# Every fourth weight chunk gets its lower part from an accumulating transfer instead of a VectorE subtraction

## The chip, the cores and the metric

The kernel runs on one core of one Trainium2 chip. The metric is the device time of one execution in microseconds (us). The core has a matrix engine (TensorE; PE for its matmuls and PEld for its weight loads in the profile), a vector engine (VectorE, DVE), a scalar engine (ScalarE, ACT), GpSimd (POOL) and SyncE (SP). SP, ACT and POOL can issue transfers (DMAs); these are carried by sixteen DMA engines between the chip's main memory and the on-chip buffers.

## The reference

The reference computes two layers of a decoder trunk on 256 rows of 2048 channels. Each layer normalizes `x`, multiplies it with one wide input matrix, feeds the pieces to four token mixers (causal pooling, latent attention with a rotary key, a gated short convolution, cross-attention to 256 memory rows), projects each mixer's output, merges the four with sigmoid gates, and adds an output projection to `x`. Cut to the parts that hold nearly all the arithmetic:

```python
for l in range(DEPTH):                       # DEPTH = 2
    h = rms_norm(x, norm_g[l])               # (256, 2048)
    proj = h @ w_in[l]                       # (2048, 18496)
    ...                                      # four mixers, with their own smaller products
    mem_kv = rms_norm(mem, mem_norm_g[l]) @ w_mem_kv[l]
    merged = gates[:, :, 0] * (y_pool @ w_branch[l, 0])
    merged = merged + gates[:, :, 1] * (y_mla @ w_branch[l, 1])
    merged = merged + gates[:, :, 2] * (y_conv @ w_branch[l, 2])
    merged = merged + gates[:, :, 3] * (y_mem @ w_branch[l, 3])
    x = x + merged @ w_out[l]
```

All inputs and outputs are 32-bit floats.

## The kernel before

Every large product is done with operands split in two. A number is written as an upper part, rounded to the type `float32r` in which TensorE takes it, and a lower part, the difference between the number and its upper part. A product of two such numbers is then formed from three matmuls (upper by upper, upper by lower, lower by upper).

The weights lie in main memory in chunks, in the order in which they are used. `wchunks` (lines 293 to 306) is a generator that brings one chunk at a time: SP loads it as 128 partitions of up to 1024 numbers into a buffer `raw` (line 303), ACT rounds it into `hi` (line 304, `A.copy`), and DVE subtracts, `lo = raw - hi` (line 305). There are four buffers for `raw`, three for `hi` and three for `lo`. The load, the rounding and the subtraction stand in a block of higher priority (`AHEAD`, 100 places in the program's order), so that they are put ahead of other work in the queues of their engines; they then wait for their buffers.

Two helpers use the chunks. `tm_block` (lines 308 to 320) has the activations as the stationary operand and the weights as the moving one; a chunk of 2 by 512 columns costs twelve matmuls, four times the lines 317, 318 and 319, and line 318 is the one that reads `lo`. `fm_block` with `fm_tile` (lines 322 to 333) has the weights stationary; a chunk of 4 by 256 columns costs eight pairs of the lines 323 and 324, and line 324 loads `lo`. A whole block is 16 k-tiles deep for most products: eight chunks in `tm_block`, four in `fm_block`. Both accumulate in `acc`, of which there are three buffers.

A run goes through 884 chunks, 442 in each layer: the key and value projection of the memory rows, the latents, the cross-attention queries, an order of attention stages written out by hand (`SEQUENCE`, line 22), then for each branch in turn the gate and branch projections (`gates`), with the pooling branch and the convolution branch between them, and the output projection. Of the 884, 836 hold 128 by 1024 numbers; 32 (the compressed keys and values) hold 128 by 576 and 16 (`uq`) hold 128 by 768.

Intermediate results of up to 128 by 1152 numbers live in buffers of the tag `t4` (lines 132 and 133), of which the pool `tp` (line 121) has seven. POOL does no arithmetic; it clears the first columns of one tile per pooling group (line 738) and per convolution half (line 783).

Of the kernel before, what the change touches and what calls it, by code (L numbers as in the profile page):

```python
# [10 lines left out]
F32 = mybir.dt.float32  # L11
F32R = mybir.dt.float32r
I32 = mybir.dt.int32
AF = mybir.ActivationFunctionType
ALU = mybir.AluOpType
AX = mybir.AxisListType

P = 128
# [92 lines left out]
def tile_hybrid_trunk(  # L111
    ctx: ExitStack, tc: tile.TileContext, x, xT, mem, memT, positions, vectors, mla_g, gate_b, weights, consts, out,
):
    nc = tc.nc
    V, A, T = nc.vector, nc.scalar, nc.tensor
# [2 lines left out]
    big = ctx.enter_context(tc.tile_pool(name="big", bufs=2))  # L118
    wp = ctx.enter_context(tc.tile_pool(name="wp", bufs=1))
    op = ctx.enter_context(tc.tile_pool(name="op", bufs=16))  # L120
    tp = ctx.enter_context(tc.tile_pool(name="tp", bufs=7))
    sp = ctx.enter_context(tc.tile_pool(name="sp", bufs=4))
    accp = ctx.enter_context(tc.tile_pool(name="accp", bufs=3, space=bass.MemoryType.PSUM))
    msp = ctx.enter_context(tc.tile_pool(name="msp", bufs=2, space=bass.MemoryType.PSUM))
# [3 lines left out]
    def nm(s):  # L128
        uid[0] += 1
        return f"{s}{uid[0]}"  # L130
# [147 lines left out]
    def step():  # L278
        if background:
            run = background.pop(0)  # L280
            if run is not None:
                run()
# [5 lines left out]
    def defer(runs, delay):  # L288
        if len(background) < delay:
            background.extend([None] * (delay - len(background)))  # L290
        background.extend(runs)

    def wchunks(l, name, c0):
        off, n, nk, kt = plan[name, c0]
        m = nk * n
        for k0 in range(0, kt, nk):
            raw = wp.tile([P, 1024], F32, tag="raw", name=nm("raw"), bufs=4)
            hi = wp.tile([P, 1024], F32R, tag="hi", name=nm("hi"), bufs=3)
            lo = wp.tile([P, 1024], F32R, tag="lo", name=nm("lo"), bufs=3)
            o = off + P * n * k0  # L300
            step()
            with tc.high_priority(AHEAD):
                nc.sync.dma_start(raw[:, :m], weights[l, o : o + P * m].rearrange("(p m) -> p m", p=P))
                A.copy(hi[:, :m], raw[:, :m])  # L304
                V.tensor_tensor(lo[:, :m], raw[:, :m], hi[:, :m].bitcast(F32), ALU.subtract)  # L305
            yield k0, nk, kt, n, *(w[:, :m].rearrange("p (k n) -> p k n", n=n) for w in (hi, lo))

    def tm_block(lhs, l, name, c0):
        ps = acc()
        for k0, nk, kt, n, hi, lo in wchunks(l, name, c0):  # L310
            for k in range(nk):
                kk = k0 + k
                o = lhs(kk // 2) if callable(lhs) else lhs[kk // 2]
                for t in range(2):
                    hh = o[:, kk % 2, 0, t * P : (t + 1) * P]
                    hl = o[:, kk % 2, 1, t * P : (t + 1) * P]
                    T.matmul(ps[:, t, :n], hh, hi[:, k, :], start=kk == 0, stop=False)  # L317
                    T.matmul(ps[:, t, :n], hh, lo[:, k, :], start=False, stop=False)  # L318
                    T.matmul(ps[:, t, :n], hl, hi[:, k, :], start=False, stop=kk == kt - 1)  # L319
        return ps  # L320
# [5 lines left out]
    def fm_block(rhs, l, name, c0):  # L326
        ps = acc()
        for k0, nk, kt, n, hi, lo in wchunks(l, name, c0):
            for j in range(2):
                for k in range(nk):  # L330
                    kk = k0 + k
                    fm_tile(ps, j, hi, lo, rhs[kk // 2], kk % 2, k, j * P, kk == 0, kk == kt - 1)
        return ps
# [396 lines left out]
    def pool_branch(l, vec, h):  # L730
# [24 lines left out]
        for b in range(2):  # L755
            sz = silu_block(h, l, OFF["pz"] + 512 * b)
            (_, _, _, _, hi, lo), = wchunks(l, "pool", 512 * b)
            for i in range(2):
                g = 2 * b + i
                ps = acc()  # L760
                for j in range(2):
                    for k in range(2):
                        fm_tile(ps, j, hi, lo, mixed[g], k, 2 * i + k, j * P, k == 0, k == 1)
                y = t2("yp").rearrange("p (n s) -> p n s", n=2)
                fm_sum(y, ps)
                for j in range(2):
                    V.scalar_tensor_tensor(
                        y[:, j, :], y[:, j, :], gcol(vec, "pool_scale", 2 * g + j), sz[:, 2 * i + j, :], ALU.mult, ALU.mult
                    )
                o = opnd()  # L770
                split(o, y)
                ys.append(o)
# [89 lines left out]
    for l in range(DEPTH):  # L862
# [45 lines left out]
        o, sz = xq, sxz  # L908
# [75 lines left out]
```

## Time and profile before

| | |
|---|---|
| Median of two runs | 2519.72 us |
| Lowest and highest | 2518.49 and 2520.94 us |
| Span of the profiled execution | 2517.2 us |
| The profiled execution's own time | the page gives only its span, so the 2.5 us to the median of the runs are counted as what lies around it |
| PE busy | 2503.9 us, 12402 matmuls |
| DVE busy, ACT busy | 1539.0 us and 1248.4 us |
| POOL busy | 1.6 us, 16 instructions |
| Transfers | 484.22 MB, 192 GB/s on average |
| Granted TensorE clock | full speed |

The page of a profile gives, for each engine, the time in which it worked and its share of the span; then groups of instructions by line of the source, with the mean duration of one instruction in ns and the idle time that the engine had just before them, with what ended that wait. `A <- B` behind a group means that A's instruction could start when B was done. In a timeline, each row has the start in us, the duration in us, the engine, the line, the operation with its output and inputs, and in square brackets the idle time before it. A matmul's row is longer than the distance to the next one, because matmuls overlap in the array. The rows themselves are shown where the prediction uses them.

### The profile page before, as it was taken

The page shows a single profiled execution, that of the slowest core. Times are in us where ns is not written, and L with a number is a line of the kernel's source. Part 1 is how long each engine was busy: PE and PEld are TensorE (multiplying, and loading weights), DVE is VectorE, ACT ScalarE, POOL GpSimd, SP SyncE. Part 2 cuts the span into 40 slices and gives each one's busy share as a digit, 9 for nine tenths or more (in the row PEclk, how much of TensorE's full clock was granted, in tenths as well). Part 3 has the DMA queues.
Part 4 walks back from the last instruction along what each step waited for, and adds up shares of the span by engine and source line. Part 5 has one row for each costly group of instructions (what it writes and reads, how often), then busy time and mean ns, then how long its engine had stood idle before and what let it go on. Part 6 is the DMA issues. An engine that isn't in the chain of part 4 may idle for free.

```text
span 2517.2 us, 32451 instructions
## 1 busy us (share of the span) xinstructions
PE 2503.9 (99%) x12402; PEld 2108.3 (84%) x12402; DVE 1539.0 (61%) x2132; ACT 1248.4 (50%) x1707; POOL 1.6 (0%) x16
## 2 busy tenths in 40 slices
PE   8999999999999999999999999999999999999999
PEld 7888888888888888888888888888888888888887
DVE  6767775566556655556474577755765565555554
ACT  7556674445444444445454566744444444444443
POOL 0000000000000000000000000000000000000000
PEclk9999999999999999999999999999999999999999
DMA  8665436655655566667655654366556655566565
GB/s 314 207 198 162 145 128 197 202 188 192 201 196 186 188 221 203 201 195 231 220 187 167 202 166 136 128 202 204 186 191 202 194 187 188 193 202 203 189 229 164
DMA packets 143676, 484.22 MB, mean 192 GB/s; under 512 B 16160, under 2 KB 17184, under 8 KB 143520
## 3 DMA queue, kind: packets, MB, share of 16 engines
q1 hardware_dynamic: 142800, 481.06, 58.5%
q8 instruction: 97, 1.59, 0.3%
q10 hardware_dynamic: 720, 1.09, 0.1%
q14 instruction: 59, 0.48, 0.1%
HBM read 477.89 MB, written 4.19 MB: 192 GB/s over the span
## 4 chain that ended last, share of the span: by engine, by line
PE 97%; DVE 1%; ACT 1%; DMA 0%; issue 0%; DVEq 0%; SPq 0%; ACTq 0%
PE acc L319 22%; PE acc L318 22%; PE acc L317 22%; PE acc L323 19%; PE acc L324 10%; PE ms L703 1%; PE ms L702 1%; PE ms L350 1%; DVE lo L305 0%; ACT junk L197 0%; PE ms L551 0%; PE ms L552 0%; PE ms L553 0%; DMA row<-in_x_dram 0%; ACT hi L304 0%; PE ms L722 0%
## 5 line engine op out<-in xcount | busy, mean ns | idle before, releaser
L305 DVE TENSOR_TENSOR lo<-raw,hi 128x1024 fp32r<-128x1024 f32 (+2 forms) x884 | 1062.4, 1202 | 869.8 <-ACT hi L304 867.0
L304 ACT CAST hi<-raw 128x1024 fp32r<-128x1024 f32 (+2 forms) x884 | 914.7, 1035 | 1179.1 <-PE acc L319 791.2
L317 PE MATMUL acc<-hi,op 128*128 128x512 f32 (+2 forms) x2496 | 962.5, 386 | 5.8 <-ACT op L392 5.7
L318 PE MATMUL acc<-lo,op 128*128 128x512 f32 (+2 forms) x2496 | 957.9, 384 | 1.7 <-DVE lo L305 1.7
L319 PE MATMUL acc<-hi,op 128*128 128x512 f32 (+2 forms) x2496 | 958.1, 384 | 0.0
L323 PE MATMUL acc<-op,hi 128*128 128x512 f32 x2080 | 736.9, 398 | 0.1
L324 PE MATMUL acc<-op,lo 128*128 128x256 f32 x2080 | 585.7, 282 | 0.0
L317 PEld LDWEIGHTS acc<-hi,op 128*128 128x128 f32 x2496 | 469.2, 188 | 95.2 <-ACT op L392 6.2
L319 PEld LDWEIGHTS acc<-hi,op 128*128 128x128 f32 x2496 | 469.0, 188 | 92.0 <-issue 1.3
L318 PEld LDWEIGHTS acc<-lo,op 128*128 128x128 f32 x2496 | 469.4, 188 | 91.1 <-DVE lo L305 2.9
L323 PEld LDWEIGHTS acc<-op,hi 128*128 128x128 f32 x2080 | 390.8, 188 | 94.3 <-DVE z L338 0.8
L324 PEld LDWEIGHTS acc<-op,lo 128*128 128x128 f32 x2080 | 392.9, 189 | 1.9 <-issue 1.3
L814 DVE TENSOR_TENSOR g<-acc,gb 128x1024 f32<-128x1024 f32 x32 | 39.2, 1224 | 12.7 <-PE acc L319 12.7
L337 ACT COPY fmt<-acc 128x512 f32<-128x512 f32 x72 | 41.4, 581 | 0.0
L815 ACT ACTIVATE g<-g 128x1024 f32<-128x1024 f32 x32 | 34.0, 1062 | 6.7 <-DVE g L814 6.7
L821 DVE TENSOR_TENSOR g<-g,acc 128x1024 f32<-128x1024 f32 x24 | 29.3, 1221 | 9.8 <-PE acc L319 9.8
L822 DVE TENSOR_TENSOR merged<-merged,g 128x1024 f32<-128x1024 f32 x24 | 29.2, 1219 | 0.0
L513 ACT ACTIVATE sm<-sm,smx,rqs 128x128 f32<-128x128 f32 (+1 forms) x32 | 17.3, 540 | 22.3 <-DVE smx L511 22.3
L494 DVE TENSOR_TENSOR z<-z,sg 128x512 f32<-128x512 f32 x32 | 22.0, 688 | 7.8 <-ACT sg L493 7.7
L197 ACT ACTIVATE junk<-acc 128x256 f32<-128x256 f32 (+2 forms) x68 | 25.2, 371 | 2.1 <-PE acc L319 1.2
L392 ACT ACTIVATE op<-ms,gt 128x256 fp32r<-128x256 f32 x32 | 15.1, 471 | 14.0 <-DVE op L393 14.0
L338 DVE TENSOR_TENSOR z<-acc,fmt 128x512 f32<-128x512 f32 x32 | 21.9, 684 | 0.0
(193 smaller groups left out, 949.1 us busy)
## 6 DMA issues: line engine op xcount, KB each, us to landing
raw<-in_weights_dram SPq DMA_DIRECT2D x836, 512.0 KB, 3.5
raw<-in_weights_dram SPq DMA_DIRECT2D x32, 288.0 KB, 2.8
gb<-in_gate_b_dram SPq DMA_DIRECT2D x32, 256.0 KB, 4.4
raw<-in_weights_dram SPq DMA_DIRECT2D x16, 384.0 KB, 3.1
mt<-in_memT_dram SPq DMA_DIRECT2D x14, 256.0 KB, 5.7
row<-in_mem_dram SPq DMA_DIRECT2D x4, 512.0 KB, 8.4
row<-in_x_dram SPq DMA_DIRECT2D x4, 512.0 KB, 8.2
xt<-in_xT_dram SPq DMA_DIRECT2D x8, 256.0 KB, 5.5
```

The source lines that it names most:

```text
L304: A.copy(hi[:, :m], raw[:, :m])
L305: V.tensor_tensor(lo[:, :m], raw[:, :m], hi[:, :m].bitcast(F32), ALU.subtract)
L317: T.matmul(ps[:, t, :n], hh, hi[:, k, :], start=kk == 0, stop=False)
L318: T.matmul(ps[:, t, :n], hh, lo[:, k, :], start=False, stop=False)
L319: T.matmul(ps[:, t, :n], hl, hi[:, k, :], start=False, stop=kk == kt - 1)
L323: T.matmul(ps[:, j, :], hi[:, k, n0 : n0 + P], o[:, half].rearrange("p a s -> p (a s)"), start=first, stop=False)
L324: T.matmul(ps[:, j, :S], lo[:, k, n0 : n0 + P], o[:, half, 0, :], start=False, stop=last)
L337: A.copy(tmp, ps[:, :, S:])
L814: V.tensor_tensor(g, pg, gb.unsqueeze(1).broadcast_to([P, 2, 512]), ALU.add)
L815: A.activation(g, g, AF.Sigmoid)
L821: V.tensor_tensor(g, g, pb, ALU.mult)
L822: V.tensor_tensor(mg, mg, g, ALU.add)
```

## The change

The chunks are counted. Where the count is a multiple of four and the chunk has the full 1024 columns, `lo` is made in another way: ACT writes the negated chunk into `lo`, which rounds it, so that it holds the negated upper part; then POOL issues a transfer that reads the same chunk from main memory a second time and adds it to what stands in `lo`. The result is again the chunk less its upper part. All other chunks keep the subtraction on DVE. The buffers are dealt out anew: three for `raw` instead of four, four each for `hi` and `lo` instead of three, and six instead of seven in the pool that holds `t4`.

```diff
-    tp = ctx.enter_context(tc.tile_pool(name="tp", bufs=7))
+    tp = ctx.enter_context(tc.tile_pool(name="tp", bufs=6))
...
+    nchunk = [0]
+
     def wchunks(l, name, c0):
...
-            raw = wp.tile([P, 1024], F32, tag="raw", name=nm("raw"), bufs=4)
-            hi = wp.tile([P, 1024], F32R, tag="hi", name=nm("hi"), bufs=3)
-            lo = wp.tile([P, 1024], F32R, tag="lo", name=nm("lo"), bufs=3)
+            raw = wp.tile([P, 1024], F32, tag="raw", name=nm("raw"), bufs=3)
+            hi = wp.tile([P, 1024], F32R, tag="hi", name=nm("hi"), bufs=4)
+            lo = wp.tile([P, 1024], F32R, tag="lo", name=nm("lo"), bufs=4)
             o = off + P * n * k0
             step()
             with tc.high_priority(AHEAD):
                 nc.sync.dma_start(raw[:, :m], weights[l, o : o + P * m].rearrange("(p m) -> p m", p=P))
                 A.copy(hi[:, :m], raw[:, :m])
-                V.tensor_tensor(lo[:, :m], raw[:, :m], hi[:, :m].bitcast(F32), ALU.subtract)
+                nchunk[0] += 1
+                if m == 1024 and nchunk[0] % 4 == 0:
+                    A.activation(lo[:, :m], raw[:, :m], AF.Copy, scale=-1.0)
+                    nc.gpsimd.dma_start(
+                        lo[:, :m], weights[l, o : o + P * m].rearrange("(p m) -> p m", p=P), accum_op=ALU.add
+                    )
+                else:
+                    V.tensor_tensor(lo[:, :m], raw[:, :m], hi[:, :m].bitcast(F32), ALU.subtract)
```

## The prediction

> **What bounds the kernel now.** I read the busy line of the page first, then the stretches of the span, then who waited for whom on PE.
>
> ```profile
> PE 2503.9 (99%) x12402; PEld 2108.3 (84%) x12402; DVE 1539.0 (61%) x2132; ACT 1248.4 (50%) x1707; POOL 1.6 (0%) x16
> 0.00:60.00 60.00, 52.60 (x217) 41.65 (x218) 39.69 (x95) 42.53 (x85) 0.20 (x4) 1.00 0.88 315
> 60.00:2500.00 2440.00, 2439.24 (x12135) 2057.07 (x12134) 1494.84 (x2034) 1203.72 (x1620) 1.43 (x12) 1.00 0.59 190
> 2500.00:2517.20 17.20, 12.02 (x54) 9.62 (x52) 4.51 (x5) 2.11 (x2) 0.00 (x0) 0.98 0.09 31
> PE acc L318 <- DVE lo L305: 1.7, 1, 1.7
> ```
>
> In the stretch rows the columns are the length, then PE, PEld, DVE, ACT and POOL with their instruction counts, the granted clock, the DMA share and GB/s. Between 60 and 2500 us PE is idle for 0.76 us of 2440; the missing 13.3 us of its whole span lie in the first 60 us (7.4) and in the tail (5.2). PE waits for `lo` once, for 1.7 us. So PE is the bound nearly everywhere, DVE has slack in every stage, and work taken from DVE can return at most a few us. Because a matmul's row is longer than the distance to the next, I also read single rows; they follow each other without a gap, twelve in 2.72 us:
>
> ```profile
> 1010.57 0.33 SPq L303 DMA_DIRECT2D raw<-in_weights_dram  x1
> 1010.75 0.39 PE L317 MATMUL acc<-hi,op 128*128 128x512 f32 x1
> 1010.95 1.05 ACT L304 CAST hi<-raw 128x1024 fp32r<-128x1024 f32 x1 [1.66 <-PE acc L319]
> 1010.98 0.39 PE L318 MATMUL acc<-lo,op 128*128 128x512 f32 x1
> 1012.04 1.23 DVE L305 TENSOR_TENSOR lo<-raw,hi 128x1024 fp32r<-128x1024 f32 x1 [1.49 <-ACT hi L304]
> 1013.67 1.05 ACT L304 CAST hi<-raw 128x1024 fp32r<-128x1024 f32 x1 [1.67 <-PE acc L319]
> ```
>
> The cast at 1010.95 waited for PE's last matmul of an older chunk: the buffers of `hi` and `lo`, not the load, set when a chunk is prepared. The next such cast comes 2.72 us later, which is the chunk's period in `tm_block`. With three buffers, the chunk cast at 1010.95 is read two periods later, its `lo` at 1010.98 + 5.44 = 1016.42; the subtraction ends at 1013.27, so 3.15 us remain unused.
>
> **The change, part by part.** *How many.* Every fourth of 884 chunks is 221. Of these, 4 in each layer fall on the chunks of 576 columns, and in the second layer, which begins at a count of 442 and so two places shifted, 4 fall on those of 768 columns: 221 - 8 - 4 = 209.
>
> *What goes and what comes on DVE and ACT.*
>
> ```profile
> L305 DVE TENSOR_TENSOR lo<-raw,hi 128x1024 fp32r<-128x1024 f32 x836 | 1022.9, 1224 | 834.7 <-ACT hi L304 832.1 <-PE acc L324 1.7
> L304 ACT CAST hi<-raw 128x1024 fp32r<-128x1024 f32 x836 | 879.8, 1053 | 1133.6 <-PE acc L319 759.6 <-PE acc L323 295.6 <-issue 45.0
> L815 ACT ACTIVATE g<-g 128x1024 f32<-128x1024 f32 x32 | 34.0, 1062 | 6.7 <-DVE g L814 6.7
> ```
>
> DVE loses 209 x 1.224 = 256 us (to 1283) and ACT gains 209 x 1.06 = 222 us (to 1470, 58% of the span), with the duration of the 128x1024 activation of line 815. Neither is the bound before or after, so the 256 us buy nothing on PE's path. Behind the negation on ACT stand the copies and sigmoids of finished blocks, up to 1.06 us later once in four chunks; a block of `acc` lasts four to eight chunks and there are three, which hides it.
>
> *How much time the new route has.* With four buffers the chunk cast at time 0 is read three periods later: 3 x 2.72 + 0.03 = 8.19 us. The cast and the negation run back to back:
>
> ```profile
> 559.00 1.05 ACT L304 CAST hi<-raw 128x1024 fp32r<-128x1024 f32 x1 [1.29 <-issue]
> 559.95 0.63 ACT L493 ACTIVATE sg<-z 128x512 f32<-128x512 f32 x1
> 564.66 1.05 ACT L304 CAST hi<-raw 128x1024 fp32r<-128x1024 f32 x1 [1.78 <-PE acc L323]
> 567.44 1.05 ACT L304 CAST hi<-raw 128x1024 fp32r<-128x1024 f32 x1 [1.73 <-PE acc L323]
> 568.39 0.58 ACT L337 COPY fmt<-acc 128x512 f32<-128x512 f32 x1
> ```
>
> An activation starts 0.95 us after the cast ahead of it, so the negation ends at 0.95 + 1.06 = 2.01. A waiting engine starts 0.04 us after ACT ends (DVE at 1012.04 after the cast that ends at 1012.00). That leaves 8.19 - 2.05 = 6.1 us **from the moment POOL may issue until the sum must have landed**. In `fm_block` the casts lie 2.78 us apart, which gives about the same or 0.2 more. The reads of all other chunks keep their order, so each late one delays PE by the full excess, and the next one, four chunks on, starts afresh: the price is 209 x (landing - 6.1).
>
> *What the landing takes.* No row of before shows a transfer issued by POOL or one that adds. The nearest rows:
>
> ```profile
> 1010.57:1011.50 0.93, 0.93 (x6) 0.78 (x5) 0.00 (x0) 0.55 (x1) 0.00 (x0) 1.00 0.02 4
> 1011.50:1013.30 1.80, 1.80 (x10) 1.49 (x9) 1.23 (x1) 0.51 (x1) 0.00 (x0) 1.00 0.83 291
> 1013.30:1014.20 0.90, 0.90 (x6) 0.74 (x5) 0.00 (x0) 0.53 (x1) 0.00 (x0) 1.00 0.00 0
> DMA to landing us min/median/max: 2.6/3.4/9.0
> row<-in_x_dram SPq DMA_DIRECT2D x4, 512.0 KB, 8.2
> pos<-in_positions_dram SPq DMA_DIRECT2D x1, 1.0 KB, 6.0
> ```
>
> The first three rows cut one raw load, issued at 1010.57, in pieces: 0.93 us until data flows, 1.80 us of data at a share of 0.83 (1.5 us of all sixteen engines), then nothing until the next load. So a load beside no other takes 2.7 us; the median is 3.4. To that I add (1) reading the destination: nothing if it overlaps with the other read, 1.5 us if it costs as much engine time again; I take 1.5. (2) Sharing: a period holds one raw load of 1.5 us, so between 0 and 1.5 are lost to it; I take 0.7, since the loads leave 0.9 us free per period. (3) Making the transfer on POOL, for which there is no row: between nothing and 3.3 us, what the 1 KB load of the positions took beyond 2.7; I take 0.5, nearer to the bulk loads. Sum 2.7 + 1.5 + 0.7 + 0.5 = **5.4 us**, 0.7 inside the 6.1. The far ends are 2.6 us and 9.0 (2.7 + 1.5 + 1.5 + 3.3; the slowest raw load and the 8.2 of the row loads, which were issued four together, say the same).
>
> The Trainium skill, in "DMA: Bandwidth & Descriptors", section "Anatomy of one DMA — SWDGE (gpsimd) path", fits a transfer issued by GpSimd as 2.0 us plus its bytes at 436 GB/s, which is an estimated 3.2 us for 512 KB and 4.4 with the bytes counted twice; by it the landing would leave 1.7 us over. Against the change speaks the Trainium skill, "Collectives: The Full Stack", Part 3: a reducing transfer reads two sources and ran at half the rate of a plain one. No row here shows it; by it term (1) is the full 1.5 that I took.
>
> *The DMA engines.* 209 x 0.524 MB is 110 MB more. At 1.5 us of all engines per chunk, once or twice, the share of 0.59 in the long stretch grows by 0.13 or 0.26, to at most 0.85. A raw load is issued when the chunk three places earlier is done with `raw`, 2.3 us after its cast, lands 3.4 us later, and is needed 8.16 us after that cast: 2.4 us of slack, with one `raw` buffer fewer. I cost it at nothing; if raw loads slow by more than 2.4 us, the excess is added to the late chunk.
>
> *POOL's queue.* The new wait stands on POOL, behind ACT. Ahead of it or behind it there are only 12 memsets:
>
> ```profile
> L738 POOL MEMSET pv<- 128x32 f32 x8 | 1.0, 125 | 1606.7 <-DVE op L342 1305.9 <-DVE merged L819 179.9 <-DVE ps L745 116.5
> L783 POOL MEMSET u<- 128x8 f32 x4 | 0.4, 106 | 341.7 <-DVE merged L822 241.2 <-DVE yp L767 100.5
> ```
>
> They wait long for a `t4` buffer because nothing hurries them. One that stands before an accumulating transfer could hold it, at worst a period of 2.72 us each, 33 us in all. The transfers are put 100 places ahead, so I take 0.
>
> *`t4` with six.* I count the live ones: two `xq`, `v2`, two of `smz`, and one `qg` or `sxz` at a time; six are enough, at nothing. Were one short, the stage waits for a release, at most a chunk each for some ten allocations: 27 us.
>
> *The start.* In the first 60 us the DMA engines are 88% busy, and five of the 209 chunks fall there; the first one's raw load must also wait for the first buffer (three instead of four). With 1.5 to 3 us of engine time each and little free, I take 6 us of 0 to 15.
>
> *Late ones.* Raw loads land between 2.6 and 9.0 us, so some sums miss 6.1 though 5.4 is usual. One in ten by 0.3 us is 21 x 0.3 = 6 us.
>
> *Sum.* 2517.2 + 2.5 around the span, + 6 + 6 = **2532 us**, 0.5% slower, which no measurement here would tell from no change (2% is the bound, 50 us). With the small terms at their ends and the gain at its limit, this case runs from 2514 to 2569.
>
> **The rivals.**
>
> *The sum lands late (slower).* Place: the wait of line 318 or 324 for `lo` in each fourth chunk. It decides from 6.1 us on; 2% is reached at 6.1 + (50 - 6)/209 = 6.3 us. For it: my 5.4 holds three taken values, and if sharing and POOL take their share in full the landing is easily 7; at 7.0 the price is 0.9 x 209 = 188 us and the time 2714; at 8.0 it is 2920. Against it: the loads now leave a third of each period free. I give 7.0 us as its likeliest.
>
> *The free DVE or the fourth buffer makes it faster.* For it: 13.3 us of PE idle. Against: 5.2 of them are the tail and most others the first load. At the very best 2506, typically 2517; never 2%.
>
> *The small buffers bite.* `t4` or a memset holds up a stage: 2532 + 27 + 33 = 2592 at worst.
>
> *The change doesn't do what it says* would be a subtraction that stays; the counts of line 305 decide it, and the time would be 2520.
>
> **How the numbers follow.** Forecast 0.52, late sum 0.41, faster-but-small 0.02, small buffers 0.03, not done 0.01, and 0.01 for a gain over 2% by something I have not seen. Of the small-buffer case two thirds stand beyond 2%. Slower by over 2%: 0.41 + 0.02 = 0.43; within 2%: 0.56; faster by over 2%: 0.01. The late sum spreads from 6.3 us to the far end of 9; up to 7.4 us (6 + 272 us, 2798) lies a good half of it, 0.24. From 2512 to 2800 the range holds 0.56 + 0.02 + 0.24 = 0.82.
>
> **What would show it.** Line 305 with 627 + 48 instructions instead of 884, a new ACT group of 209 at about 1.06 us, a POOL transfer group of 209 with its median to landing: under 6.1 if I am right. PE's waits then hold little for `lo`; if the late sum wins, PE's idle time, or gaps between its rows, appear before line 318 once in four chunks, of the size landing less 6.1, and the chain of waits shows these transfers. The prediction is wrong if an adding transfer costs more than twice a plain one, or POOL takes over 1 us to make it.

## The result: 10% slower

| | before | after |
|---|---|---|
| Median of the runs | 2519.72 us | 2770.28 us (2764.36 to 2776.2) |
| Ratio to before | | 1.0997, 95% interval 1.0939 to 1.1056 |
| Span of the profiled execution | 2517.2 us | 2762.6 us |
| PE busy, PE idle | 2503.9 and 13.3 us | 2577.9 and 184.7 us |

The time lies inside the range of 2512 to 2800, but the case I called likeliest, no change, did not happen: the first rival did. The sum lands late, and PE waits for it. The range had been drawn over both cases, so that it holds the time is no merit of the sum behind the forecast.

In the changed kernel the lines have new numbers: the raw load 303 is 305, the cast 304 is 306, the subtraction 305 is 314, and the readers of `lo`, 318 and 324, are 327 and 333; the negation is 309 and the adding transfer 310. These are lines of its page: the span, the busy line, the two DMA queues that carry the weights (packets, MB, and the packets' time as a share of all sixteen engines), the chain by engine (the work that ended last, followed back from the end), the groups that the prediction named, and the two kinds of transfer with KB and median us to landing.

```profile
span 2762.6 us, 32891 instructions
PE 2577.9 (93%) x12402; PEld 2126.1 (77%) x12402; DVE 1295.4 (47%) x1923; ACT 1440.6 (52%) x1916; POOL 182.3 (7%) x225
q1 hardware_dynamic: 142800, 481.06, 50.4%
q0 software_dynamic: 30096, 109.59, 23.6%
PE 52%; DMA 38%; ACT 5%; issue 4%; DVE 1%; ACTq 0%; DVEq 0%; POOLq 0%
L314 DVE TENSOR_TENSOR lo<-raw,hi 128x1024 fp32r<-128x1024 f32 (+2 forms) x675 | 806.7, 1195 | 1135.2 <-ACT hi L306 1134.4
L310 POOL DMA_DIRECT2D lo<-in_weights_dram x209 | 180.6, 864 | 2565.4 <-ACT lo L309 2367.4
L309 ACT ACTIVATE lo<-raw 128x1024 fp32r<-128x1024 f32 x209 | 221.4, 1059 | 183.8 <-PE acc L327 176.9
raw<-in_weights_dram SPq DMA_DIRECT2D x836, 512.0 KB, 4.5
lo<-in_weights_dram POOLq DMA_DIRECT2D x209, 512.0 KB, 7.6
```

The change was made as described: 675 subtractions, 209 negations, 209 transfers. They land 7.6 us after POOL begins to issue them, not 5.4. Transfers now hold 38% of the chain that ended last. What PE waited for (us in total, times, longest), and the same two stretches of the span that were shown of before:

```profile
PE acc L327 <- DMA lo<-in_weights_dram: 105.5, 73, 7.1
PE acc L333 <- DMA lo<-in_weights_dram: 66.6, 50, 2.4
```

```profile
0.00:60.00 60.00, 40.18 (x140) 30.29 (x141) 27.73 (x64) 35.40 (x66) 2.94 (x7) 0.89 0.83 270
60.00:2500.00 2440.00, 2297.71 (x11232) 1902.65 (x11231) 1166.88 (x1769) 1293.14 (x1738) 161.61 (x198) 0.99 0.74 213
```

172 us of waiting for the adding transfers stand where before had 1.7 us for the subtraction. In the long stretch PE is idle for 142 us instead of 0.76, and in the first 60 us it gets through 140 matmuls instead of 217. Now one stall, in the timeline of PE, with the granted clock behind it (the third column from the right in the windows):

```profile
1012.16 0.39 PE L328 MATMUL acc<-hi,op 128*128 128x512 f32 x1
1012.39 0.39 PE L326 MATMUL acc<-hi,op 128*128 128x512 f32 x1
1014.63 0.50 PE L327 MATMUL acc<-lo,op 128*128 128x512 f32 x1 [1.86 <-DMA lo<-in_weights_dram]
1014.97 0.40 PE L328 MATMUL acc<-hi,op 128*128 128x512 f32 x1
...
1016.41 0.63 PE L327 MATMUL acc<-lo,op 128*128 128x512 f32 x1
1016.83 0.63 PE L328 MATMUL acc<-hi,op 128*128 128x512 f32 x1
```

```profile
1014.00:1015.00 1.00, 0.37 (x2) 0.32 (x3) 1.00 (x2) 0.21 (x1) 0.00 (x0) 1.00 0.97 369
1015.00:1016.00 1.00, 1.00 (x6) 0.76 (x5) 0.97 (x2) 0.00 (x0) 0.00 (x0) 0.90 1.04 356
1016.00:1017.00 1.00, 1.00 (x4) 0.81 (x3) 0.26 (x1) 0.00 (x0) 0.00 (x0) 0.50 1.14 315
1018.00:1019.00 1.00, 1.00 (x4) 0.72 (x4) 0.00 (x0) 0.65 (x1) 0.00 (x0) 0.50 0.82 315
1019.00:1020.00 1.00, 1.00 (x5) 0.84 (x4) 0.00 (x0) 1.00 (x2) 0.29 (x1) 0.90 0.42 160
```

The first read of `lo` in a fourth chunk waits 1.86 us; some 1.2 us later the granted clock falls to half for 3.4 us, and matmuls follow each other every 0.43 us instead of every 0.23. Over the whole trace I count 21 such stretches ahead of the tail (17 of 3.41 us, 4 of 6.83 us, which at half speed lose 43 us); before has none ahead of its tail.

**Where the 250 us are.** The profiled execution is 245 us longer. PE idle: 184.7 - 13.3 = 171 us. PE busy longer: 2577.9 - 2503.9 = 74 us, of which 43 are the halved clock. The other 31 I put down to the stalls themselves: 143 of the 209 sums came late, the row before a stall no longer overlaps its successor (0.39 us long, 0.23 apart), and the first row after it is slower (0.50). 143 x 0.16 is 23 us of the 31; this is argued from the rows, not tried, and the other 8 us stay open.

### The profile page after: what moved, and what is told of

Its sections match the earlier page's. It is cut to its first block, busy times and chain, and to the rows that moved or that the text cites. A ratio compares the mean times of both kernels' runs of the same rounds, so it can differ in the third digit from the quotient of the medians.

```text
span 2762.6 us, 32891 instructions
## 1 busy us (share of the span) xinstructions
PE 2577.9 (93%) x12402; PEld 2126.1 (77%) x12402; DVE 1295.4 (47%) x1923; ACT 1440.6 (52%) x1916; POOL 182.3 (7%) x225
## 3 DMA queue, kind: packets, MB, share of 16 engines
q1 hardware_dynamic: 142800, 481.06, 50.4%
## 4 chain that ended last, share of the span: by engine, by line
PE 52%; DMA 38%; ACT 5%; issue 4%; DVE 1%; ACTq 0%; DVEq 0%; POOLq 0%
DMA lo<-in_weights_dram 35%; PE acc L327 13%; PE acc L328 12%; PE acc L326 12%; PE acc L332 7%; PE acc L333 4%; ACT lo L309 4%; DMA raw<-in_weights_dram 2%; ACT hi L306 1%; DVE lo L314 1%; PE ms L712 1%; PE ms L711 1%; PE ms L359 0%; PE ms L731 0%; PE ms L560 0%
## 5 line engine op out<-in xcount | busy, mean ns | idle before, releaser
L314 DVE TENSOR_TENSOR lo<-raw,hi 128x1024 fp32r<-128x1024 f32 (+2 forms) x675 | 806.7, 1195 | 1135.2 <-ACT hi L306 1134.4
L327 PE MATMUL acc<-lo,op 128*128 128x512 f32 (+2 forms) x2496 | 981.8, 393 | 106.0 <-DMA lo<-in_weights_dram 105.5
L326 PE MATMUL acc<-hi,op 128*128 128x512 f32 (+2 forms) x2496 | 974.1, 390 | 6.0 <-ACT op L401 5.8
L328 PE MATMUL acc<-hi,op 128*128 128x512 f32 (+2 forms) x2496 | 969.5, 388 | 0.0
L327 PEld LDWEIGHTS acc<-lo,op 128*128 128x128 f32 x2496 | 476.2, 191 | 236.8 <-DMA lo<-in_weights_dram 147.0
L333 PE MATMUL acc<-op,lo 128*128 128x256 f32 x2080 | 593.9, 286 | 66.6 <-DMA lo<-in_weights_dram 66.6
L326 PEld LDWEIGHTS acc<-hi,op 128*128 128x128 f32 x2496 | 475.5, 191 | 99.9 <-ACT op L401 6.4
L328 PEld LDWEIGHTS acc<-hi,op 128*128 128x128 f32 x2496 | 476.0, 191 | 90.2 <-DVE op L402 0.7
L310 POOL DMA_DIRECT2D lo<-in_weights_dram x209 | 180.6, 864 | 2565.4 <-ACT lo L309 2367.4
L309 ACT ACTIVATE lo<-raw 128x1024 fp32r<-128x1024 f32 x209 | 221.4, 1059 | 183.8 <-PE acc L327 176.9
```

The costliest lines, as they stand in the source:

```text
L309: A.activation(lo[:, :m], raw[:, :m], AF.Copy, scale=-1.0)
L310: nc.gpsimd.dma_start(lo[:, :m], weights[l, o : o + P * m].rearrange("(p m) -> p m", p=P), accum_op=ALU.add)
L333: T.matmul(ps[:, j, :S], lo[:, k, n0 : n0 + P], o[:, half, 0, :], start=False, stop=last)
```

## The experiments

**Theory:** the sum lands later than its chunk is read. The landing is long because the transfer reads two sources and shares the DMA engines with the raw loads. So a shorter landing, or a longer budget (the time from POOL's issue to PE's first read of the sum), must each give back most of the time. **Rivals:** the new deal of buffers costs it; the extra traffic makes raw loads late; the missing fourth `raw` buffer does.

### The buffers alone

```diff
-                if m == 1024 and nchunk[0] % 4 == 0:
+                if False:
```

> The changed kernel with its buffers (three raw, four hi, four lo, six t4), but with the VectorE subtraction for every chunk. Late sum (theory): the 250 us come from the wait for the accumulating transfers alone, so 2520 us, between 2514 and 2530. Buffers (rival): one raw or t4 buffer fewer costs part of the 250 us, so over 2570. Traffic (rival): as the theory, since the second read is gone.

Measured 2521.75 us, ratio 1.0006 [0.9997, 1.0015]. The busy line of its page is that of before within 3 us:

```profile
PE 2507.1 (99%) x12402; PEld 2110.0 (84%) x12402; DVE 1537.5 (61%) x2132; ACT 1247.5 (49%) x1707; POOL 1.6 (0%) x16
```

Three `raw`, four `hi` and `lo`, and six in the pool of `t4` cost nothing as long as DVE subtracts. The rival of the buffers is out.

### The whole route beside the kernel, with nobody reading its result

The buffers of `raw`, `hi` and `lo` are those of before.

```diff
-                    A.activation(lo[:, :m], raw[:, :m], AF.Copy, scale=-1.0)
+                    ex = wp.tile([P, 1024], F32R, tag="ex", name=nm("ex"), bufs=1)
+                    A.activation(ex[:, :m], raw[:, :m], AF.Copy, scale=-1.0)
...
-                        lo[:, :m], weights[l, o : o + P * m]..., accum_op=ALU.add
+                        ex[:, :m], weights[l, o : o + P * m]..., accum_op=ALU.add
...
-                else:
-                    V.tensor_tensor(lo[:, :m], raw[:, :m], hi[:, :m].bitcast(F32), ALU.subtract)
+                V.tensor_tensor(lo[:, :m], raw[:, :m], hi[:, :m].bitcast(F32), ALU.subtract)
```

> The subtraction on VectorE for every chunk, with four raw, three hi and three lo as before (t4 six), and beside it the same 209 negations on ACT and the same 209 accumulating transfers on POOL, into a buffer of their own that nobody reads. Late sum: the traffic alone costs little, 2530 us, between 2518 and 2550, though the transfers land as late as in the change (7 to 8 us). Traffic: most of the 250 us remain, over 2650. Buffers: 2520.

Measured 2546.16 us, 1.0101 [1.0086, 1.0116]. Busy line and transfers of its page:

```profile
PE 2517.4 (99%) x12402; PEld 2113.2 (83%) x12402; DVE 1536.2 (60%) x2132; ACT 1439.9 (57%) x1916; POOL 182.8 (7%) x225
raw<-in_weights_dram SPq DMA_DIRECT2D x836, 512.0 KB, 4.9
ex<-in_weights_dram POOLq DMA_DIRECT2D x209, 512.0 KB, 6.6
```

All 209 negations and transfers run, raw loads take 4.9 us to land, and yet only 25 us are lost. The transfers land after 6.6 us, sooner than the 7 to 8 that I expected and the 7.6 of the changed kernel, so the traffic is not quite the same. With that reserve, traffic, ACT's extra work and POOL together are a tenth of the 250; the rest needs PE to wait for the sum.

### The transfer without its addition

The transfer overwrites `lo` with the raw weights; everything waits as it did.

```diff
-                        lo[:, :m], weights[l, o : o + P * m]..., accum_op=ALU.add
+                        lo[:, :m], weights[l, o : o + P * m]...
```

> The changed kernel, but the transfer on POOL copies the chunk instead of adding it, so the addition is left out and lo holds the chunk itself. Late sum: a packet should take about 0.16 us as those of raw do, not 0.33, so 1.5 us of engine time and some sharing go; median landing 5.5 to 6.0 instead of 7.6 us, which is inside the 6.3 (fm_block) and 7.1 us (tm_block) that the changed kernel's trace shows between issue and first use; time 2535 us, between 2522 and 2570. Buffers: 2770. Traffic: half of the excess, 2640.

Measured 2559.81 us, 1.0155 [1.0135, 1.0175]. Queue and transfer on its page, and the wait:

```profile
q0 software_dynamic: 30096, 109.59, 13.7%
lo<-in_weights_dram POOLq DMA_DIRECT2D x209, 512.0 KB, 5.6
```

```profile
PE acc L327 <- DMA lo<-in_weights_dram: 24.2, 17, 4.5
PE acc L333 <- DMA lo<-in_weights_dram: 0.5, 2, 0.3
```

The same packets and bytes take 0.137 x 2555.7 / 209 = 1.68 us of all sixteen engines per transfer, against 0.236 x 2762.6 / 209 = 3.12 us with the addition. The landing falls from 7.6 to 5.6 us, and 210 of the 250 us come back.

### No raw loads beside it

One chunk is loaded at the start and stands in for all raw loads.

```diff
+    once = cp.tile([P, 1024], F32, name="once")
+    nc.sync.dma_start(once, weights[0, 0 : P * 1024].rearrange("(p m) -> p m", p=P))
...
-            raw = wp.tile([P, 1024], F32, tag="raw", name=nm("raw"), bufs=3)
+            raw = once
...
-                nc.sync.dma_start(raw[:, :m], weights[l, o : o + P * m].rearrange("(p m) -> p m", p=P))
```

> The changed kernel without any raw load: all 884 chunks are cast or negated from one buffer that is loaded once, so the upper parts of all weights are left out; the 209 adding transfers and all engines' instructions stay. The run that kept the 209 raw loads still had them beside the transfers (1.4 us of raw packets while a transfer was on its way). If sharing is the missing part: first data after 1.6 us, 3.1 us of packets, landing at 4.8 to 5.3 us, no wait of PE, 2525 us, between 2517 and 2545. If the adding transfer is slow by itself: landing over 6.3 us and over 2600.

Measured 2545.22 us, 1.0107 [1.0073, 1.0141]: 20 us above what I expected and at the upper end of its range, 225 below the changed kernel. Queue and transfer of its page, then the waits (its lines stand one further down), then its first 60 us:

```profile
q0 software_dynamic: 30096, 109.59, 25.7%
lo<-in_weights_dram POOLq DMA_DIRECT2D x209, 512.0 KB, 5.4
```

```profile
PE acc L327 <- ACT hi L307: 11.9, 1, 11.9
PE acc L328 <- DMA lo<-in_weights_dram: 10.1, 8, 5.0
PE acc L334 <- DMA lo<-in_weights_dram: 2.0, 4, 0.9
```

```profile
0.00:60.00 60.00, 42.62 (x162) 34.15 (x163) 28.82 (x69) 36.87 (x66) 3.80 (x8) 0.94 0.68 195
```

An adding transfer with no weight load beside it lands in 5.4 us, with 0.257 x 2547.1 / 209 = 3.13 us of engine time. That is the 5.4 that I had predicted *with* sharing. PE then waits 12 us for sums instead of 172. Compared matmul by matmul, the profiled execution is 14 us behind before at 60 us, where the single load has held up the first chunk (11.9 us) and the clock is 0.94, and 30 us behind at the end. Of the 15 us that come later, 7 are waits for sums; the rest I did not trace.

### Only the raw loads of the fourth chunks (a miss)

```diff
+            nchunk[0] += 1
+            own = m == 1024 and nchunk[0] % 4 == 0
-            raw = wp.tile([P, 1024], F32, tag="raw", name=nm("raw"), bufs=3)
+            raw = wp.tile([P, 1024], F32, tag="raw", name=nm("raw"), bufs=2) if own else once
...
+                if own:
+                    nc.sync.dma_start(raw[:, :m], ...)
```

> The changed kernel without the raw loads of all chunks but the 209: the other 675 chunks are cast from one buffer that is loaded once, so their weights are left out; all engines' instructions stay. Late sum with sharing as the missing part of its landing: the transfer has the DMA engines nearly to itself, starts to move data after 1.6 us, needs 3.1 us for its packets and lands after 4.8 to 5.3 us; no wait of PE, 2525 us, between 2517 and 2545. Rival (adding or making the transfer on POOL is slow by itself): landing stays over 6.5 us and the time over 2620.

Measured 2675.82 us, 1.0617 [1.0596, 1.0639], 150 us over what I expected. From its page:

```profile
lo<-in_weights_dram POOLq DMA_DIRECT2D x209, 512.0 KB, 6.9
```

Three raw loads of four are gone, and the transfer still takes 6.9 us. The one that is left is issued when the cast and the negation are done with its buffer, and in 203 of 209 cases that is between 0.5 us before and 1.0 us after POOL issues; in the packet times 1.5 us of raw data still flow between POOL's issue and the sum's last data. The loads that the edit took away are worth 0.7 us of the landing (7.6 to 6.9), the one that it left is worth 1.5 (6.9 to the 5.4 of the run without any load). The run without any load is the one that measures sharing.

### One more buffer for `lo`, and one for `raw`

The fifth `lo` lengthens the budget by one period of 2.72 us. To make room, four smaller pools lose a buffer each (`pT`, `gb`, the one sized by `PB`, and `t2`).

```diff
-            raw = wp.tile([P, 1024], F32, tag="raw", name=nm("raw"), bufs=3)
+            raw = wp.tile([P, 1024], F32, tag="raw", name=nm("raw"), bufs=4)
...
-            lo = wp.tile([P, 1024], F32R, tag="lo", name=nm("lo"), bufs=4)
+            lo = wp.tile([P, 1024], F32R, tag="lo", name=nm("lo"), bufs=5)
```

> The changed kernel with four raw, four hi and five lo buffers, paid for with one buffer fewer each of pT, gb, pb and t2, as with five hi and five lo. There, ScalarE's casts waited 716 us for raw loads. If the raw buffers are what is left there: 2560 us, between 2530 and 2600. If the landing itself (8.0 us in the median there) is still too late with one period more, or the small buffers cost: 2640 or more.

Measured 2587.06 us, 1.0270 [1.0253, 1.0287]. Transfer on its page, waits, and the two stretches:

```profile
lo<-in_weights_dram POOLq DMA_DIRECT2D x209, 512.0 KB, 8.0
```

```profile
PE acc L327 <- DMA lo<-in_weights_dram: 40.3, 25, 7.9
PE acc L333 <- DMA lo<-in_weights_dram: 3.0, 5, 1.5
```

```profile
0.00:60.00 60.00, 38.55 (x140) 29.11 (x141) 27.25 (x63) 33.63 (x60) 3.81 (x8) 0.90 0.86 276
60.00:2500.00 2440.00, 2404.91 (x11915) 2018.11 (x11914) 1239.01 (x1831) 1381.31 (x1822) 173.05 (x210) 0.99 0.80 229
```

Here the landing is *longer* than in the changed kernel, 8.0 us, and 183 of the 250 us come back. It is the distance between landing and first read that decides, not the landing. Matmul by matmul, the profiled execution is 19 us behind before at 60 us, as the changed kernel is, and 68 us at the end. Of the 49 us that come later, 28 are waits of PE for sums that are still late; the pools that were cut, which the next run prices, are a further part.

### The pools that pay for it

Line 314 makes `lo` for all chunks, with the buffers of the changed kernel but for the four pools.

```diff
-PB = 2
+PB = 1
...
-        return tp.tile([P, 512], F32, tag="t2", name=nm(s), bufs=7)
+        return tp.tile([P, 512], F32, tag="t2", name=nm(s), bufs=6)
...
-                if m == 1024 and nchunk[0] % 4 == 0:
+                if False:
...
-            pT = tp.tile([P, 512], F32, tag="pT", name=nm("pT"), bufs=2)
+            pT = tp.tile([P, 512], F32, tag="pT", name=nm("pT"), bufs=1)
...
-            gb = tp.tile([P, 512], F32, tag="gb", name=nm("gb"), bufs=2)
+            gb = tp.tile([P, 512], F32, tag="gb", name=nm("gb"), bufs=1)
```

> VectorE subtraction for every chunk with the change's buffers (three raw, four hi, four lo, six t4) and one buffer fewer each of pT, gb, pb and t2: the control for the two runs that paid for buffers with these. If they cost nothing: 2522 us; if they are what is left in those runs: 2560 or more.

Measured 2533.89 us, 1.0059 [1.0036, 1.0081]: 12 us over the run with the changed kernel's buffers alone, and between the two values that were expected.

### Five `hi` and five `lo`, three `raw` (a miss)

The same four pools pay.

```diff
-            hi = wp.tile([P, 1024], F32R, tag="hi", name=nm("hi"), bufs=4)
-            lo = wp.tile([P, 1024], F32R, tag="lo", name=nm("lo"), bufs=4)
+            hi = wp.tile([P, 1024], F32R, tag="hi", name=nm("hi"), bufs=5)
+            lo = wp.tile([P, 1024], F32R, tag="lo", name=nm("lo"), bufs=5)
```

> The changed kernel with five hi and five lo buffers instead of four; paid for with one buffer fewer each of pT, gb, pb and t2. The same transfers, the same ACT work, three raw and six t4 as in the change; but a chunk may be prepared one period (2.72 us) earlier. Late sum: 9 to 9.8 us of time against a landing of 5.4 to 9.7: nearly all waits go, 2540 us, between 2520 and 2590 (the small buffers may hold up a stage). Buffers or traffic: 2770 stays, at least 2700.

Measured 2651.68 us, 1.0522 [1.0498, 1.0547], where 2540 was expected. Its waits of ACT and of PE:

```profile
ACT hi L306 <- DMA raw<-in_weights_dram: 716.1, 259, 6.3
```

```profile
PE acc L327 <- DMA lo<-in_weights_dram: 67.2, 50, 6.9
PE acc L333 <- DMA lo<-in_weights_dram: 12.5, 18, 1.8
```

With the fifth pair the cast could start a period earlier, but it then waits for the raw load: with three `raw` buffers the limit moves from `lo` to `raw`, and only 119 us come back. In the run with four `raw` and five `lo` that wait is 16 us instead of 716. The two runs differ in `hi` too (five here, four there), but the wait shows that the fourth `raw` buffer matters as soon as `lo` has five.

### A fourth `raw` buffer alone

`pT` and `gb` pay for it.

```diff
-            raw = wp.tile([P, 1024], F32, tag="raw", name=nm("raw"), bufs=3)
+            raw = wp.tile([P, 1024], F32, tag="raw", name=nm("raw"), bufs=4)
```

> The changed kernel with four raw buffers instead of three, and one buffer fewer of pT and gb. Late sum by hi and lo: the negation waits mostly for a lo buffer, not for raw, so only a little goes: 2745 us, between 2700 and 2775. Raw (rival): the late raw loads set the start of the negation, and the fourth buffer brings it to 2620 or less.

Measured 2769.54 us, 1.0989 [1.0967, 1.1011]. No gain: with four `lo` the raw load is not the limit, as the prediction had it, though I expected some 25 us by then. The rival of the missing `raw` buffer is out.

### Every eighth chunk

```diff
-                if m == 1024 and nchunk[0] % 4 == 0:
+                if m == 1024 and nchunk[0] % 8 == 0:
```

> The changed kernel with every eighth instead of every fourth chunk by the new route: 105 transfers instead of 209. Late sum: each late one costs by itself, 1.2 us per transfer on average, so half of 250 us: 2645 us, between 2620 and 2670. Traffic that saturates (rival): the loss falls by far more than half, under 2590.

Measured 2666.43 us, 1.058 [1.0558, 1.0602]: 147 us for 105 transfers, 1.40 us each, against 250.6 / 209 = 1.20. The landing is 7.8 us. Half the extra traffic does not make the single sum cheaper, so it is not the mean load on the DMA engines that makes it late, but what it meets on its own way.

### Half the columns

The upper 512 columns go by the transfer, the lower 512 by DVE.

```diff
-                    A.activation(lo[:, :m], raw[:, :m], AF.Copy, scale=-1.0)
+                    A.activation(lo[:, 512:], raw[:, 512:], AF.Copy, scale=-1.0)
...
-                        lo[:, :m], weights[l, o : o + P * m]..., accum_op=ALU.add
+                        lo[:, 512:], weights[l, o : o + P * m]...[:, 512:], accum_op=ALU.add
...
+                    V.tensor_tensor(lo[:, :512], raw[:, :512], hi[:, :512].bitcast(F32), ALU.subtract)
```

> The changed kernel, but a fourth chunk gets only its second 512 columns by the new route, and the first 512 by a VectorE subtraction; 209 transfers of 256 KB. Late sum: 1.55 us of packets instead of 3.1, landing at 5.0 to 5.8 us instead of 7.6, inside the 6.3 and 7.1 us that there are: 2545 us, between 2525 and 2580. If the fixed part of the route (making, issue) were what is late: over 2650.

Measured 2534.75 us, 1.0069 [1.0046, 1.0092]. The time from issue to landing of the tile `lo`, and PE's wait:

```profile
DMA to landing us min/median/max: 3.6/5.4/8.5
```

```profile
PE acc L328 <- DMA lo<-in_weights_dram: 11.8, 7, 3.6
```

The same number of transfers, negations and waits, half the bytes: 5.4 us, and the stalls are gone but for seven. The negation of half a chunk is also 0.43 us shorter (0.631 against 1.059), which lengthens the budget by as much; the 2.2 us of landing are the larger part. No version run here that moves the subtraction beats before.

### The transfers from the 25th chunk on

```diff
-                if m == 1024 and nchunk[0] % 4 == 0:
+                if m == 1024 and nchunk[0] % 4 == 0 and nchunk[0] > 24:
```

> The changed kernel, but the first 24 chunks (six transfers) keep the VectorE subtraction. The traces put the changed kernel 29 us behind at its 20th chunk. If that is a cost of the start of its own, beside transfers that land late everywhere: 2738 us, between 2728 and 2748. If these six cost what the others cost (1.2 us each): 2763 us, at least 2755.

Measured 2743.06 us, 1.0894 [1.0873, 1.0915]. Its first 60 us:

```profile
0.00:60.00 60.00, 52.64 (x208) 41.20 (x209) 37.87 (x94) 42.95 (x85) 0.20 (x4) 0.97 0.86 307
```

PE is as busy there as in before (52.60), with 208 matmuls for its 217 at a clock of 0.97, and the whole is 27 us shorter than the changed kernel: the six transfers of the start cost 4.5 us each, the other 203 1.1 us each.

## Why the sum of the prediction went wrong

**What it got right.** PE was the bound, and the work taken from DVE returned nothing. The count of 209 and the durations held: 1.059 us per negation, line 314 x675. The small terms held too: buffers and `t4` cost nothing, and POOL starts 0.29 us after the negation in all but three of the 209 transfers (2.3 us at most), so its queue holds up next to nothing. The three `raw` buffers did not bind with four `lo`. The mechanism of the late sum was described as it happened, with PE stalled ahead of lines 327 and 333, at 143 of the 209 chunks. The traffic, with the extra work of ACT and POOL, cost 25 us.

**The step that failed** is *what the landing takes*: 2.7 + 1.5 + 0.7 + 0.5 = 5.4 us, said to lie 0.7 inside the budget. The measured terms:

- Reading the destination, taken as 1.5: 3.12 - 1.52 = 1.6 us of engine time (a raw load costs 0.504 x 2762.6 / 918 = 1.52, with 481.06 MB counted as 918 chunks). Right. The landing falls by 2.0 when it is left out. The Trainium skill, "Collectives: The Full Stack", Part 3, says that a reducing transfer runs at half the rate of a copy because it reads two sources; the 3.12 against 1.52 agree.
- Making the transfer on POOL, taken as 0.5: alone it lands in 5.4 us (the run without loads), which leaves 5.4 - 2.7 - 1.6 = 1.1 as a remainder. POOL's instruction takes 0.86 us, against 0.33 for SP's. The Trainium skill, "DMA: Bandwidth & Descriptors", section "Anatomy of one DMA — SWDGE (gpsimd) path", gave an estimated 3.2 us for the plain transfer and 4.4 with the bytes doubled; the runs have 5.4 for the adding one alone, a microsecond more than the second estimate. The plain one took 3.4 us at the least, near the first estimate, and 5.6 in the median beside the loads.
- Sharing with raw loads, taken as 0.7: 7.6 - 5.4 = 2.2 us. This is the largest error, above the 1.5 that I had set as its upper end. I reasoned that the loads leave 0.9 us free in each period. But ACT frees `raw` when it has cast and negated the chunk, so a raw load is issued just as the transfer is: in 205 of the 209 cases between 0.5 us before and 1.0 us after POOL starts. The median landing is 7.8 us with such a load ahead (76 transfers), 7.4 with one just behind (129) and 6.4 with neither (4). And a sum that needs 3.1 us of all engines cannot fit between loads that come every 2.7 us and take 1.5.

So the error of 2.2 us in the landing is 1.5 of sharing, 0.6 of making and 0.1 of reading. The prediction's own signs of error missed this: an adding transfer costs 3.12 / 1.68 = 1.9 times a plain one of POOL (2.05 times a raw load), and POOL takes 0.86 us to make it, so neither sign shows clearly, while the term that failed, sharing, had no sign.

**The budget** was roughly right for the cast-first order and too small for the other. ACT's timeline and POOL's show both orders (the row of SP is the raw load issued beside the first of these transfers):

```profile
1004.12 1.05 ACT L306 CAST hi<-raw 128x1024 fp32r<-128x1024 f32 x1 [3.25 <-PE acc L332]
1005.08 1.05 ACT L309 ACTIVATE lo<-raw 128x1024 fp32r<-128x1024 f32 x1
...
1018.36 1.06 ACT L309 ACTIVATE lo<-raw 128x1024 fp32r<-128x1024 f32 x1 [4.15 <-PE acc L327]
1019.32 1.03 ACT L306 CAST hi<-raw 128x1024 fp32r<-128x1024 f32 x1
```

```profile
1006.15 0.33 SPq L305 DMA_DIRECT2D raw<-in_weights_dram  x1
1006.42 0.86 POOL L310 DMA_DIRECT2D lo<-in_weights_dram  x1 [12.24 <-ACT lo L309]
1019.71 0.86 POOL L310 DMA_DIRECT2D lo<-in_weights_dram  x1 [12.42 <-ACT lo L309]
```

In `tm_block` the last reader of `lo` (line 327) comes one matmul ahead of the last reader of `hi` (328), so the buffer of `lo` comes free first, and ACT negates *before* it casts. From the start t of that matmul: it ends at t + 0.39, ACT waits 0.04 and takes 1.06, POOL starts 0.29 later (1006.13 to 1006.42, where I had 0.04), at t + 1.78. The chunk is read at t + 0.68 + 3 x 2.72 = t + 8.84, so 7.06 us remain. In `fm_block`, cast first, the stall-free rows give 6.3. Hence my price of 209 x (landing - 6.1) would have made 313 us of a landing of 7.6. The PE waits sum to 172, as some 144 of the 209 chunks are of the kind with 7.06.

**Two terms were missing or small.** The halved clock after stalls, 43 us, was in no case of mine; my rival's price counted only the waiting. The start was set at 6 us (0 to 15) and its six transfers cost 27: there the DMA engines are 83% busy, PE stalls for up to 7.1 us, and the clock is 0.89.

**The chances.** I put 0.41 on the late sum, and the far ends (2.6 to 9.0 us) held the truth, so the range did too; but its upper end was set where it takes in half of the late sums, and the time lies only 30 us inside it. And three of the four terms had no row in the trace, and for two of them I took values in the lower half of their bounds. The sum came out close to the budget. With a landing of 5.4 against 6.1 and ends at 2.6 and 9.0 the late sum deserved more than half.

## What to carry to other kernels

Price an asynchronous step by its latency under the load that its own release sets free, and set that against the distance to its first reader; both a plain transfer (5.6 us) and an adding one without neighbours (5.4) cost 1 to 2% here, while the adding one beside loads (7.6) cost 10%. Where the bound engine has no idle time, as here, relieving another engine has next to nothing to win, and a late arrival is paid on the bound engine, with the clock on top. If such a step must be kept, give its destination and its source one more buffer each (8.0 us of landing, 2.7% lost), or halve it (0.7% lost).

## What the runs showed of the hardware that I had not expected

- **The clock falls after short stalls.** In the changed kernel, of PE's idle gaps of 1.8 to 2.1 us 11 of 18 came with a stretch at half the clock, of those over 3 us 6 of 6, of those from 0.3 to 1.5 us 0 of 61; between these, from 1.5 to 1.8 and from 2.1 to 3 us, it was 2 of 26 and 2 of 4. The limit is not sharp: with four `raw` buffers it was 8 of 17 between 1.8 and 2.1 us, and in the run with the transfers off the path three of the four gaps between 1.0 and 1.5 us came just ahead of such a stretch too (two stretches). The Trainium skill, "TensorE: Matmul & The Clock Gate", Part 1, puts the throttle behind an idle window of about 3.4 us. The length of the stretches, 3.41 us or twice that, fits this window; the gaps that bring them on are shorter here.
- **A POOL transfer behind a raw load starts its data later.** In the packet times the first data of an adding transfer flow 1.6 us after POOL starts in the median of the 105 cases where the last raw load was issued 1 to 2 us ahead, and 1.6 in the run without loads; where a raw load was issued less than 0.5 us ahead, in 76 of the 209, the median is 2.6.
